# Low halves of the down-projection weights: an accumulating transfer in place of a subtraction on VectorE

## The chip, the cores and the metric

The kernel runs on one core of a Trainium2 chip. The metric is the device time of one execution in microseconds. Each time below is either that, or a time inside the one execution that the hardware profiler recorded. The engines are named as the profile names them: PE is the matrix engine (TensorE), with PEld for its weight loads, DVE is VectorE, ACT is ScalarE, POOL is GpSimd, and SP is the engine whose queue issues the transfers.

## The reference, cut to what matters

A two-layer network works on 256 rows of 1024 columns in float32. Each layer is a feed-forward, a mixer and a second feed-forward, each added to the residual `h`:

```
def swiglu(x, w_gu, w_down):              # w_gu [1024, 5632], w_down [2816, 1024]
    g, u = jnp.split(x @ w_gu, 2, axis=-1)
    return (jax.nn.silu(g) * u) @ w_down

for layer in range(2):
    h = h + 0.5 * swiglu(rmsnorm(h, ffn1_norm[layer]), ffn1_wgu[layer], ffn1_wd[layer])
    hn = rmsnorm(h, mix_norm[layer])
    h = h + (even_mixer if layer % 2 == 0 else odd_mixer)(hn, ...)
    h = h + 0.5 * swiglu(rmsnorm(h, ffn2_norm[layer]), ffn2_wgu[layer], ffn2_wd[layer])
return rmsnorm(h, final_norm)
```

So there are four feed-forwards, and each has one down-projection `w_down`. The change concerns the weights of these four products alone.

## The kernel before, in words

**Split products.** The matrix engine takes operands in a form of float32 that it handles in one pass (`F32R`) and that carries fewer bits. So each operand is split into a high and a low part, and a product is made of three: high times high, high times low, low times high. `mm3` issues them (L185, L186, L188); L186 is the one that reads the low part of the weights. For the weights the split has two steps, in `split`: ACT copies `raw` into `hi`, which rounds it (L103), and DVE writes `lo = raw - hi` (L104). The activations go through the same two lines under the tile name `aT`.

**Streaming.** All weights come from HBM in groups of 128 partitions by 2048 columns of float32, 1 MB each. `load_group` issues the transfer on SP (L123 for the gate and up weights, two transfers a group; L125 for a down-projection group, one transfer; L117 for the mixers' input projections), and then the split in pieces of 1024 columns. Three buffers hold `raw`, five hold `hi` and five hold `lo`. A `raw` buffer comes free when the group's split has read it, a `hi` or `lo` buffer when the last product with the group is done.

**Units.** A feed-forward is cut into 11 chunks of 256 of its 2816 hidden columns. For chunk j an a-unit computes gate and up (24 products of 512 columns for each half of the rows, two weight groups), applies `silu` on ACT (`ffs`, L359) and the product on DVE (`ffa`, L361); three chunks of products later two transposes on PE (L201) and another split give `aT`. A b-unit multiplies `aT` with the down-projection group of chunk j (12 products for each half of the rows) and sums in PSUM (`acc`). The order is a0, a1, b0, a2, b1, a3, b2 and so on. The 256 rows are two halves of 128, and the second half follows the first by between one and two units (`LAG`), so both use a weight group while it is in SBUF. In the middle of a feed-forward PE works through this sequence, where the number is the half of the rows: 1: a(j), 0: a(j+1), 1: b(j-1), 0: b(j), 1: a(j+1), 0: a(j+2), and so on.

**Order.** Each engine takes its instructions in a fixed order, and an instruction that waits holds up those behind it. A planner sets the order when the program is built. It goes by the order of the code and by its own reckoning of when operands and buffers will be ready, so a step that the code has later can come earlier. A few steps (transposes, norms, mixer chains) are put by hand between the products (`defer`). At the end of a feed-forward or mixer the norm needs two small operations on POOL (L223, L224).

**Buffers of a down-projection group.** Groups follow each other as a, a, b, a, a, b. With five `hi` and five `lo` buffers, the group of b(j) takes the buffers of the fifth group before it, which is the first of the two groups of a(j). They come free when the second half of the rows is halfway through a(j).

The function that the diff touches, and what calls it:

Of the kernel before, what the change touches and what calls it, by code (L numbers as in the profile page):

```python
# [25 lines left out]
EPS = 1e-6  # L26
# the first units (unit, first chunk): their loads in small pieces
FINE = {(0, 0): ((0, 1), (1, 2), (2, 4)), (0, 4): ((0, 2), (2, 4)), (1, 0): ((0, 2), (2, 4)), (1, 4): ((0, 2), (2, 4))}
# how many units the second half of the rows is behind
LAG = 1.5  # L30
# delays, in 512-column chunks of the products
FIRST = 1
# [3 lines left out]
STEPS = (2, 2, 10, 5, 3, 3, 6, 7, 3, 1, 1, 30, 10, 10, 9, 8, 3, 2, 10, 3, 3, 2, 9, 2)  # L36
# columns of the output scaled on the scalar engine
CUT = 320
# columns per splitting instruction beside the mixers
MSTEP = 512  # L40
# [12 lines left out]
def hybrid_kernel(ctx: ExitStack, tc: tile.TileContext, I, out):  # L53
# [31 lines left out]

# [1 line left out]
    xf = I["x"].rearrange("b (t p) d -> (b t) p d", p=P)  # L87
# [11 lines left out]

# [1 line left out]
    def split(src2, hi2, lo2):  # L101
        """src = hi + lo exactly, both carried by one-pass products"""
        S.activation(hi2, src2, AF.Copy)  # L103
        V.tensor_tensor(out=lo2, in0=src2, in1=hi2.bitcast(F32), op=ALU.subtract)  # L104
# [3 lines left out]

    def load_group(src, a, b, fine=False, step=1024, hook=None):
        """one streamed weight group, seen as [128, a, b] with a * b <= 2048; hook is told of each part to be split"""  # L110
        n = a * b
        raw = wpool.tile([P, n], F32, tag="raw", bufs=3, name=nm("raw"))
        if isinstance(src, list):
            rv = raw.rearrange("p (a b) -> p a b", a=a)
            c = 0
            for x in src:
                nc.sync.dma_start(rv[:, :, c:c + x.shape[2]], x)  # L117
                c += x.shape[2]
        elif len(src.shape) == 4:
            rv = raw.rearrange("p (a c b) -> p a c b", a=src.shape[1], c=src.shape[2])  # L120
            for a0, a1 in (fine or [(0, a)]):
                for c in range(src.shape[2]):
                    nc.sync.dma_start(rv[:, a0:a1, c, :], src[:, a0:a1, c, :])  # L123
        else:
            nc.sync.dma_start(raw.rearrange("p (a b) -> p a b", a=a), src)  # L125
        hi = wpool.tile([P, n], F32R, tag="hi", bufs=5, name=nm("hi"))
        lo = wpool.tile([P, n], F32R, tag="lo", bufs=5, name=nm("lo"))
        step = 512 if fine else step

        def splits():  # L130
            for c in range(0, n, step):
                e = min(n, c + step)
                with after(hook(c // step) if hook else None):
                    split(raw[:, c:e], hi[:, c:e], lo[:, c:e])
        if hook is None or hook(None):
            splits()
        else:
            defer(FIRST, splits)
        v = "p (a b) -> p a b"
        return hi.rearrange(v, a=a), lo.rearrange(v, a=a)  # L140
# [3 lines left out]
    def defer(n, fn):  # L144
        """runs fn after n more chunks of the products, or when its result is needed"""
        pend.append([n, fn])
# [15 lines left out]
    def chain(gen):  # L162
        """a chain of small steps between the chunks of the products; it yields how many chunks
        to let pass, or what has to hold, before the next step"""
        wait = [None]

        def step():
            if wait[0] is not None and not wait[0]():
                defer(1, step)
                return  # L170
            wait[0] = None
            v = next(gen, StopIteration)
            if v is StopIteration:
                return
            if callable(v):
                wait[0] = v
                v = 1
            defer(v, step)
        step()

    def mm3(outs, xT, k, wk, start, stop):
        """outs: list of (psum, column slice) sharing the stationary chunk k; wk: (hi, lo) views [128, cols]"""
        xh, xl = xT
# [12 lines left out]
    def transpose_into(src, n, xT, k0, w=None):  # L196
        """n (<= 4) chunks of 128 columns of src -> xT[:, k0 : k0 + n] in split form, times w by channel"""
        if w is None:
# [38 lines left out]
    def norm0(w):  # L237
        """the first norm, among the splits of the first weights"""
        xT = new_T(0)
# [26 lines left out]
    def norm(t, w, wait=None):  # L266
        """transposed, split, weighted residual; the row scale is left to the evacuations"""
        xT = new_T(t)
        state["xT"][t] = None

        def tr():
            # neighbouring chunks lie in different banks, which the engines then read at one time
            pt = [ps_tile(tag=x) for x in ("ps", "acc", "ps", "acc")]
# [23 lines left out]

    # the table set of the feed-forward is there before its first use
    S.activation(mh4[:, 0:1], one, AF.Silu)
    G.memset(mh4, -0.5)  # L300

    def after(ins):
        """keeps the accumulation groups of one PSUM bank in turn"""
        return tc.issue_after(ins.ins) if ins is not None else nullcontext()
# [4 lines left out]

# [1 line left out]
    def final_open():  # L311
# [3 lines left out]
    def final_part(t, n):  # L315
        """half of the row: its share of the mean square, and the product with the weights; then the scale"""
        if n == 0:
# [19 lines left out]

# [1 line left out]
    def ffn_units(wgu, wd, nxt, layer0=False):  # L339
# [31 lines left out]
        def b_unit(j):  # L371
            def load():
                return [load_group(wdv[j], 2, D)]

            def run(t, w):
# [13 lines left out]
                if j == NCHUNK - 1 and nxt is None:  # L389
                    # one half is done while the other is still in the products  # L390
                    for n in range(2):
# [20 lines left out]

# [1 line left out]
    def proj_unit(w_in, cols, body):  # L414
        """some columns of an input projection: pieces (first column, width) side by side"""
        wv = w_in.rearrange("(k p) n -> p k n", p=P)
# [42 lines left out]
    def logsigmoid(dst, z, pre, w, bufs=1):  # L459
        """min(z, 0) - log(1 + exp(-|z|))"""  # L460
        e = mt(pre + "e", [P, w], bufs)
# [5 lines left out]
    def head_rms_scale(psO, name):  # L467
        """per-head 1/rms of [128, 4, 128]"""
        sq = mt("sq", [P, 4, P], 1)
# [13 lines left out]

# [1 line left out]
    def even_units(w_in, w_lr_up, b_lr, w_out, nxt):  # L485
# [29 lines left out]
        def gla_chain(t, gl):  # L515
# [12 lines left out]
            yield STEPS[2]  # L528
            # cumulative sums by constant matrices (1/16 folded in)
            pb = ps_tile(tag="acc")  # L530
# [17 lines left out]
            yield has(t, "q", "k")  # L548
            # q exp(b - bmid), k exp(bmid - b), q exp(b), k exp(bend - b)
            q, k = d["q"], d["k"]  # L550
# [16 lines left out]
            yield STEPS[4]  # L567
            # masked scores, transposed: partitions s, columns l
            for hh in range(2):
# [181 lines left out]

# [1 line left out]
    def odd_units(w_in, prm, w_out, nxt):  # L753
# [33 lines left out]
        def softplus8():  # L787
            """8 softplus(-lambda), with log(1 + e) good for small e too"""
            lam = C["lp"][:, 2, :]
# [22 lines left out]
        def conv(x, pt, t, tag):  # L812
            """causal depthwise convolution of transposed scores; channels on partitions"""
            cb = C[x + "cb"]
# [74 lines left out]
        def ml_chain(t, u):  # L889
# [31 lines left out]
            else:  # L921
                # queries weighted by what is left of the first chunk's state
                pw = ps_tile(tag="acc")
# [15 lines left out]
            else:  # L939
                yield lambda: "mc1" in C  # L940
            # numerators, and denominators in the column of ones
            hm = mt("hm", [P, 4, P], 2)
# [42 lines left out]
        def lru_chain(t, u):  # L985
# [19 lines left out]
            S.activation(f2(r), f2(a), AF.Square)  # L1005
            # 1 - a^2 = tanh(y) (1 + a^2)
            V.scalar_tensor_tensor(out=f2(ta), in0=f2(r), scalar=1.0, in1=f2(ta), op0=ALU.add, op1=ALU.mult)
# [41 lines left out]

# [1 line left out]
    for layer in range(2):  # L1051
# [31 lines left out]

    # the second half of the rows follows LAG units behind, so that each half's small work is under the other's products
    order = [0, 1, 0, 0, 1]
# [11 lines left out]
def _constants():  # L1097
    """constants that depend on shapes alone"""
    c = {}
# [43 lines left out]
def _chan(a):  # L1143
    """[n, 512] -> [128, 4, n]: channels on partitions"""
    return np.ascontiguousarray(a.reshape(a.shape[0], 4, P).transpose(2, 1, 0))
# [29 lines left out]
```

## Time and profile before

| | |
|---|---|
| device time, median of 2 runs (lowest to highest) | 1004.94 us (1004.37 to 1005.51) |
| span of the profiled execution, first to last instruction | 1004.4 us |
| busy time of PE | 989.5 us, 99% |
| busy time of DVE | 585.9 us, 58% |
| busy time of ACT | 529.0 us, 53% |
| busy time of POOL | 22.5 us, 2% |
| busy share of the 16 DMA engines | 55.1% for the loads |

The span is one execution. It lies 0.5 us under the median of the device times and 1.1 us under the higher of the two, and a device time contains a span and the little that lies around it. "Busy" is the time in which an engine had an instruction under way. The engines work beside each other, so their busy times don't add up to the span, and what bounds the kernel is read from who waits for whom. In a row of groups the columns are line, engine, operation, tile written and tiles read, shapes, count, then total busy us and mean ns, then the idle time of the engine just before these instructions and what ended it.

### The profile page before, as it was taken

To read this page: it belongs to the slowest core of one execution; us is meant where nothing else is said; L and a number is where in the kernel's file an instruction comes from. 1 tells how busy PE (TensorE), PEld (TensorE's weight loads), DVE (VectorE), ACT (ScalarE), POOL (GpSimd) and SP (SyncE) were. 2 spreads that over 40 slices of the span, in tenths; PEclk is the share of its full clock that TensorE was granted. 3 is DMA by queue.
4 is the path that set the end of the run, shared out by engine and by line. 5 is a ranking of instruction groups with operands and counts; after the bars stand their busy time and mean duration, and the time that the engine had idled before them with its cause. 6 is when DMAs were issued, how large, how long until landed. Compare 5 with 4: busy or idle time off the path is not lost.

```text
span 1004.4 us, 12334 instructions
## 1 busy us (share of the span) xinstructions
PE 989.5 (99%) x4704; PEld 813.0 (81%) x4704; DVE 585.9 (58%) x945; ACT 529.0 (53%) x877; POOL 22.5 (2%) x54
## 2 busy tenths in 40 slices
PE   7999999999999999999999999999999999999997
PEld 5888888887888888888888888888988888888885
DVE  6654545576576654545465455545878765555453
ACT  7544444484455644444454445444998764444442
POOL 1000000000100000000000000000000000000000
PEclk9999999999999999999999999999999999999999
DMA  8956564645247565565656565655334656656521
GB/s 276 311 177 200 172 206 149 190 132 172 95 168 227 163 210 192 176 202 170 207 168 205 163 205 161 206 167 153 127 126 139 218 168 209 207 166 205 165 96 42
DMA packets 129796, 178.01 MB, mean 177 GB/s; under 512 B 8756, under 2 KB 104900, under 8 KB 129736
## 3 DMA queue, kind: packets, MB, share of 16 engines
q1 hardware_dynamic: 129736, 177.22, 55.1%
q8 instruction: 37, 0.61, 0.2%
q14 instruction: 23, 0.19, 0.1%
HBM read 176.15 MB, written 1.05 MB: 176 GB/s over the span
## 4 chain that ended last, share of the span: by engine, by line
PE 92%; ACT 3%; DMA 2%; DVE 1%; issue 1%; SPq 0%; POOLq 0%; POOL 0%; ACTq 0%
PE ps L185 19%; PE ps L188 19%; PE ps L186 19%; PE acc L185 9%; PE acc L188 9%; PE acc L186 9%; PE ps L201 2%; DMA raw<-in_ffn_wgu_dram 2%; ACT hi L103 1%; DVE lo L104 1%; DMA cum<-in_c_cum_dram 0%; PE acc L615 0%; PE acc L618 0%; PE acc L279 0%; PE acc L481 0%
## 5 line engine op out<-in xcount | busy, mean ns | idle before, releaser
L104 DVE TENSOR_TENSOR lo<-raw,hi 128x1024 fp32r<-128x1024 f32 (+3 forms) x400 | 398.8, 1029 | 262.4 <-ACT hi L103 260.8
L103 ACT ACTIVATE hi<-raw 128x1024 fp32r<-128x1024 f32 (+3 forms) x400 | 342.7, 900 | 244.5 <-PE ps L188 138.1
L185 PE MATMUL ps<-hi,Th 128*128 128x512 f32 (+3 forms) x928 | 364.2, 392 | 1.3 <-ACT Th L215 1.3
L188 PE MATMUL ps<-hi,Tl 128*128 128x512 f32 (+3 forms) x928 | 357.3, 385 | 0.0
L186 PE MATMUL ps<-lo,Th 128*128 128x512 f32 (+3 forms) x928 | 356.6, 384 | 0.0
L185 PEld LDWEIGHTS ps<-hi,Th 128*128 128x128 f32 x928 | 175.3, 189 | 34.7 <-ACT Th L215 1.7
L188 PEld LDWEIGHTS ps<-hi,Tl 128*128 128x128 f32 x928 | 175.0, 189 | 34.6 <-issue 0.2
L186 PEld LDWEIGHTS ps<-lo,Th 128*128 128x128 f32 x928 | 175.5, 189 | 31.8 <-DVE lo L104 0.2
L185 PE MATMUL acc<-hi,aT 128*128 128x512 f32 x352 | 142.7, 405 | 0.0
L186 PE MATMUL acc<-lo,aT 128*128 128x512 f32 x352 | 138.9, 394 | 0.0
L359 ACT ACTIVATE ffs<-ps,rs 128x256 f32<-128x256 f32 x88 | 41.8, 474 | 154.0 <-PE ps L188 154.0
L188 PE MATMUL acc<-hi,aT 128*128 128x512 f32 x352 | 111.0, 395 | 0.0
L361 DVE SCALAR_TENSOR_TENSOR ffa<-ps,rs,ffs 128x256 f32<-128x256 f32 x88 | 42.4, 481 | 92.4 <-ACT ffs L359 92.4
L188 PEld LDWEIGHTS acc<-hi,aT 128*128 128x128 f32 x352 | 66.1, 188 | 15.1
L186 PEld LDWEIGHTS acc<-lo,aT 128*128 128x128 f32 x352 | 66.5, 189 | 13.8
L185 PEld LDWEIGHTS acc<-hi,aT 128*128 128x128 f32 x352 | 66.5, 189 | 13.4
L104 DVE TENSOR_TENSOR aT<-ps,aT 128x256 fp32r<-128x256 f32 x88 | 36.8, 418 | 7.5 <-ACT aT L103 7.5
L103 ACT ACTIVATE aT<-ps 128x256 fp32r<-128x256 f32 x88 | 32.8, 373 | 11.6 <-PE ps L201 11.6
L201 PEld LDWEIGHTS ps<-ident,ffa 128*128 128x128 f32 x176 | 24.6, 140 | 12.3 <-DVE ffa L361 0.6
L201 PE MATMUL ps<-ident,ffa 128*128 128x128 f32 x176 | 33.6, 273 | 0.1
L215 ACT ACTIVATE Th<-ps,nw 128x128 fp32r<-128x128 f32 x56 | 21.0, 375 | 12.9 <-PE ps L279 11.3
L185 PE MATMUL acc<-hi,Th 128*128 128x512 f32 x64 | 25.3, 399 | 0.0
(269 smaller groups left out, 535.9 us busy)
## 6 DMA issues: line engine op xcount, KB each, us to landing
raw<-in_ffn_wgu_dram SPq DMA_DIRECT2D x168, 512.0 KB, 4.9
raw<-in_ffn_wd_dram SPq DMA_DIRECT2D x44, 1024.0 KB, 4.9
raw<-in_e_w_in_dram SPq DMA_DIRECT2D x13, 1024.0 KB, 5.0
raw<-in_o_w_in_dram SPq DMA_DIRECT2D x9, 1024.0 KB, 5.1
raw<-in_e_w_out_dram SPq DMA_DIRECT2D x4, 1024.0 KB, 5.0
raw<-in_o_w_out_dram SPq DMA_DIRECT2D x4, 1024.0 KB, 5.0
raw<-in_ffn_wgu_dram SPq DMA_DIRECT2D x14, 256.0 KB, 6.3
rope<-in_c_rope_dram SPq DMA_DIRECT2D x4, 256.0 KB, 3.9
```

Source lines behind the costliest of these rows:

```text
L103: S.activation(hi2, src2, AF.Copy)
L104: V.tensor_tensor(out=lo2, in0=src2, in1=hi2.bitcast(F32), op=ALU.subtract)
L185: T.matmul(ps, xh[:, k, :], wk[0][:, sl], start=start, stop=False)
L186: T.matmul(ps, xh[:, k, :], wk[1][:, sl], start=False, stop=False)
L188: state["mm"] = T.matmul(ps, xl[:, k, :], wk[0][:, sl], start=False, stop=stop)
L201: T.transpose(pt[:, i * P:(i + 1) * P], src[:, i * P:(i + 1) * P], ident)
L215: last = S.activation(hi, p_, AF.Copy, scale=w[:, k:k + 1])
L359: state["act"] = S.activation(s, ps[:, :FCH], AF.Silu, scale=rs)
L361: state["dve"] = V.scalar_tensor_tensor(out=a, in0=ps[:, FCH:], scalar=rs, in1=s, op0=ALU.mult, op1=ALU.mult)
```

## The change

For the 44 down-projection groups `load_group` gets `accum=True`. ACT then copies the whole group of 2048 columns into `hi` in one instruction, and writes `lo = -hi` with a second copy of the same size. A transfer issued on POOL's queue then adds `raw` to `lo` in place, from SBUF to SBUF, so that `lo` becomes `raw - hi`. DVE has no part in it. The other weight groups are split as before. Comments and docstrings also leave the file; nothing else changes.

```
-    def load_group(src, a, b, fine=False, step=1024, hook=None):
+    def load_group(src, a, b, fine=False, step=1024, hook=None, accum=False):
...
         hi = wpool.tile([P, n], F32R, tag="hi", bufs=5, name=nm("hi"))
         lo = wpool.tile([P, n], F32R, tag="lo", bufs=5, name=nm("lo"))
         step = 512 if fine else step
+        if accum:
+
+            S.activation(hi, raw, AF.Copy)
+            S.activation(lo, hi.bitcast(F32), AF.Copy, scale=-1.0)
+            G.dma_start(lo, raw, accum_op=ALU.add)
+            v = "p (a b) -> p a b"
+            return hi.rearrange(v, a=a), lo.rearrange(v, a=a)
...
         def b_unit(j):
             def load():
-                return [load_group(wdv[j], 2, D)]
+                return [load_group(wdv[j], 2, D, accum=True)]
```

## The prediction

> **What bounds the kernel now.** I read the profile's page first, for the busy times, the queues and the chain that ended last.
>
> ```profile
> PE 989.5 (99%) x4704; PEld 813.0 (81%) x4704; DVE 585.9 (58%) x945; ACT 529.0 (53%) x877; POOL 22.5 (2%) x54
> ...
> q1 hardware_dynamic: 129736, 177.22, 55.1%
> ...
> PE 92%; ACT 3%; DMA 2%; DVE 1%; issue 1%; SPq 0%; POOLq 0%; POOL 0%; ACTq 0%
> ...
> raw<-in_ffn_wd_dram SPq DMA_DIRECT2D x44, 1024.0 KB, 4.9
> ```
>
> PE is busy for 989.5 of 1004.4 us, and the chain that ended last runs through PE for 92%. DVE, which the change relieves, is 1% of that chain. All idle time of PE together is 14.9 us, 1.5% of the span, so relief for another engine can't win 2% even if it removed all of it. The question is only whether the change makes PE wait. I take 2% (20 us) as what a measurement of this kernel tells from no change.
>
> Next I read the groups by shape and one period in the middle of the last feed-forward: the sums of the stretch, and in order of time ACT, DVE, SP and PE.
>
> ```profile
> L104 DVE TENSOR_TENSOR lo<-raw,hi 128x1024 fp32r<-128x1024 f32 x256 | 305.7, 1221 | 233.2 <-ACT hi L103 232.0 <-DMA raw<-in_ffn_wd_dram 1.0
> L103 ACT ACTIVATE hi<-raw 128x1024 fp32r<-128x1024 f32 x256 | 260.9, 1053 | 214.7 <-PE ps L188 120.1 <-PE acc L188 86.1 <-DMA raw<-in_ffn_wgu_dram 3.6
> L103 ACT ACTIVATE hi<-raw 128x512 fp32r<-128x512 f32 x136 | 76.8, 627 | 16.7 <-PE ps L188 9.5 <-DMA raw<-in_ffn_wgu_dram 5.4 <-issue 1.6
> ```
>
> ```profile
> 845.00:861.94 16.94, 16.94 (x80) 13.88 (x77) 8.63 (x10) 7.41 (x10) 0.00 (x0) 1.00 0.59 187
> ```
>
> ```profile
> 850.76 2.01 ACT L103 ACTIVATE hi<-raw 128x1024 fp32r<-128x1024 f32 x2 [3.44 <-PE ps L188]
> 853.48 0.48 ACT L359 ACTIVATE ffs<-ps,rs 128x256 f32<-128x256 f32 x1 [0.71 <-PE ps L188]
> 853.85 2.00 ACT L103 ACTIVATE hi<-raw 128x1024 fp32r<-128x1024 f32 x2
> ...
> 861.98 1.06 ACT L103 ACTIVATE hi<-raw 128x1024 fp32r<-128x1024 f32 x1 [2.33 <-PE acc L188]
> ...
> 867.70 2.01 ACT L103 ACTIVATE hi<-raw 128x1024 fp32r<-128x1024 f32 x2 [3.44 <-PE ps L188]
> ```
>
> ```profile
> 851.85 2.36 DVE L104 TENSOR_TENSOR lo<-raw,hi 128x1024 fp32r<-128x1024 f32 x2 [3.03 <-ACT hi L103]
> 854.13 0.48 DVE L361 SCALAR_TENSOR_TENSOR ffa<-ps,rs,ffs 128x256 f32<-128x256 f32 x1
> 854.93 2.36 DVE L104 TENSOR_TENSOR lo<-raw,hi 128x1024 fp32r<-128x1024 f32 x2 [0.33 <-ACT hi L103]
> ```
>
> ```profile
> 854.24 0.37 SPq L125 DMA_DIRECT2D raw<-in_ffn_wd_dram  x1
> 857.32 9.39 SPq L123 DMA_DIRECT2D raw<-in_ffn_wgu_dram  x4
> ```
>
> ```profile
> 847.84 0.39 PE L185 MATMUL ps<-hi,Th 128*128 128x512 f32 x1
> ...
> 853.28 0.39 PE L185 MATMUL ps<-hi,Th 128*128 128x512 f32 x1
> ```
>
> ```profile
> 855.32 0.38 PE L201 MATMUL ps<-ident,ffa 128*128 128x128 f32 x2
> ```
>
> ```profile
> 861.91 0.48 PE L185 MATMUL acc<-hi,aT 128*128 128x512 f32 x1
> 862.23 0.39 PE L186 MATMUL acc<-lo,aT 128*128 128x512 f32 x1
> ```
>
> The period is 16.94 us (850.76 to 867.70), and PE has no gap in it. In it a down-projection group b(j) goes this way. At 850.76 ACT begins its high part; what ended ACT's wait is a product (L188), because the group's `hi` and `lo` buffers are those that the first half of a(j) gives back then. The transfer of the next down-projection group starts at 854.24, just after the two subtractions ended (851.85 + 2.36 = 854.21), which marks these splits as b(j)'s. PE reads the low part first at 862.23. So `lo` is ready 8.0 us early. That slack, not DVE's busy time, is what the change spends.
>
> **The change part by part.** *Removed:* two subtractions of 1.22 us per group on DVE, 44 x 2.44 = 107 us of busy time. They lie beside PE's products, so the end gains nothing.
>
> *ACT.* From the rows of 512 and 1024 columns, 1024 more columns cost 2 x (1.053 - 0.627) = 0.85 us, so one of 2048 costs 1.053 + 0.85 = 1.9 us. Two 1024-column copies (2.01 us) become two of 1.9 us, 3.8 in all: ACT has 1.8 us more per group and its share of the period goes from 7.41 to 9.2 of 16.94 us, which fits. From 850.76 the negated copy is done at 854.57. Behind it on ACT waits `ffs`, which ran at 853.48 and now runs at 854.57, 1.09 us later. Its result goes through `ffa` (done at 854.61) to the transposes at 855.32, a cover of 0.71 us. What shows through is between nothing and 1.09 - 0.71 = 0.38 us a period. I take nothing, because the planner orders by readiness: it had the splits at 853.85 ahead of work that the code has earlier, and it can put one product ahead of the transposes. The splits behind move to about 855.0; the buffer for them is free and their group is read a period later.
>
> *The transfer.* It may start at 854.57 and must have landed by 862.23, a cover of 7.66 us. No transfer of this kind is in the trace, so I bound it by the loads.
>
> ```profile
> DMA to landing us min/median/max: 4.6/4.9/7.7
> ```
>
> ```profile
> L224 POOL TENSOR_TENSOR rs<-rm,mh 128x1 f32<-128x1 f32 x12 | 6.6, 553 | 1.0
> ...
> L224 POOL TENSOR_TENSOR rs<-rm,mh 128x4 f32<-128x4 f32 x6 | 6.1, 1013 | 0.5
> ```
>
> ```profile
> POOL rm L223 <- ACT junk L234: 628.3, 11, 179.0
> ```
>
> The loads kept 16 engines busy for 55.1% of 1004.4 us with 177.22 MB, so 3.12 us per MB, and 3.3 us for a group of 128 x 2048 x 4 bytes = 1.05 MB. A load of that size lands after 4.9 us, so 1.6 us are start and completion. An adding transfer reads two operands and writes one. Counted once, like a load, it lands after 4.9 us; with both operands read at that price after 1.6 + 6.5 = 8.2; with the write on top after 11.4. I take two reads, since a load's price contains its write. Issuing it on POOL costs between 0 and 1.0 us, by the POOL rows; I take 0.55, the smaller operation. Sharing the engines with a load costs between 0 and 3.3 us, one load's worth; I take 0, since 3.12 us per MB was measured on packets that already share. Together 8.2 + 0.55 = 8.7 us from the negated copy, against a cover of 7.66: PE waits 1.1 us at the first product with `lo`. It waits in order, so the other half's products stand behind it, and nothing gives the time back: the buffers of the next group come free by PE's own progress.
>
> By the Trainium skill, page "Collectives: The Full Stack", section "The bandwidth ceiling: the fold count and why AG ≠ RS ≠ AR", a reducing transfer runs at half the rate of a copy because each chunk needs two source reads, not because the addition costs anything; that is a rule against this change, and no run here shows it yet.
>
> *The `raw` buffer* is given back when the transfer has landed, at 854.57 + 8.7 = 863.3 in place of 854.21. If the next down-projection group loads into the same buffer it lands at 863.3 + 4.9 = 868.2, when its split would begin at 867.70, plus the 1.1 us that PE lost by then: just in time. The loop of one buffer, 3.8 + 8.7 + 4.9 + 0.37 for the issue = 17.8 us, stays under the new period of 18.0. SP's queue is in order, so the two loads at 857.32 and after may stand behind the wait for that buffer; their groups are split from 861.98 and 870.8 on (one period after 853.85), so this costs nothing while the transfer is under about 11 us.
>
> *POOL's queue* has only the norms' small operations, and it sat waiting for ACT's sums of squares for 628.3 us. A norm can now stand behind a transfer that waits for ACT's two copies: between nothing and 3.8 us at each of the 12 in the row of 128x1, 46 us. I take nothing, because a steady period has no POOL operation (0.00 in the sums above) and only a transfer beside a norm could hold one up.
>
> *Sum.* Of 44 groups, the first of each feed-forward is split beside a norm and its cover is another, so I count 40: 40 x (8.7 - 7.66) = 42 us. Made against the profiled execution: 1004.4 + 42 = 1046; it lies 0.5 us under the median of the runs, so 1047.
>
> **The rivals.**
> *The transfer hides (not slower).* Place: the wait of L186 in each b-unit. It decides at 7.66 us from the negated copy to the landing. For it: counted once it takes 4.9 + 0.55 = 5.5 us, and reading SBUF may be quicker than HBM. Also, the planner may foresee a late `lo` and put the other half's a-unit first: that has 24 products of weights that are already split, 5.4 us of cover more (847.84 to 853.28, the first products of two a-units that follow each other). Against it: two operands. The time is then the old one, 1005 us.
> By the Trainium skill, page "DMA: Bandwidth & Descriptors", section "Anatomy of one DMA — SWDGE (gpsimd) path", a transfer issued from POOL's queue costs about 2.0 us plus its bytes at 436 GB/s. With both operands' bytes that is an estimate of 6.8 us, by which the transfer would hide; for one load's bytes it gives 4.4 us, where the trace's loads from SP's queue took 4.9.
>
> *ACT alone costs.* The transfer hides, but `ffs` pushes the transposes by 0.38 us in 40 periods: 15 us, 1020 us. For it: copies of 1.9 us can't be interrupted. Against it: the planner.
>
> *Far longer transfer.* At 11.4 us with write and reads apart, and up to 3.3 more beside a load: 40 x (11.4 - 7.66) = 150 to 40 x (14.7 - 7.66) = 282 us, so 1155 to 1287 us. The `raw` loop gives the same order: with the longest landing in the trace, 7.7 us, it is 20.6 us, 3.7 more than the period, 1152 us. For it: the engines are already busy for 0.59 of a period. Against it: this needs each byte to cost three times.
>
> *Something gets faster.* Only PE's 14.9 us of idle time are there, so over 2% needs what no row shows.
>
> **How the numbers follow.** Late by 0.5 to 3.5 us in 40 periods, 1025 to 1145 us: 0.43, the likeliest, with 1047 as its value. Hidden: 0.37. ACT alone: 0.07. Far longer: 0.11. Faster by over 2%: 0.02. The range from 1003 to 1145 holds the first three and leaves out 0.13. Slower by over 2% is 0.43 + 0.11 = 0.54, within 2% is 0.37 + 0.07 = 0.44, faster 0.02.
>
> **What would show it.** The forecast: PE idle before L186 with `acc`, ended by a DMA, about 40 times and 1 us each; a period of about 18 us; a new queue with 44 transfers, landing 8 to 9 us after issue. Two ACT copies of 1.9 us in a row and `ffs` about 1.1 us later in its period show the ACT step. If the landing is under 7.5 us, or the order on PE has changed so that the a-unit runs ahead of the b-unit, the forecast is wrong and the time is the old one. If idle time ended by a DMA stands before L103 in place of L186, the `raw` loop bounds and not the cover.

## The result and the profile after

The changed kernel takes 1066.18 us (median of 2 runs, 1065.18 to 1067.17) against 1004.94 us: a ratio of 1.061, 95% interval 1.058 to 1.064, so 61 us more. The profiled execution of it has a span of 1063.4 us, 59.0 more than before.

The rows of the page that answer to those shown of before: the busy times, the queues, the chain that ended last by engine, and the landing of the transfers.

```profile
PE 1014.2 (95%) x4704; PEld 817.9 (77%) x4704; DVE 486.0 (46%) x857; ACT 603.8 (57%) x877; POOL 60.3 (6%) x98
...
q1 hardware_dynamic: 129736, 177.22, 49.2%
q0 software_dynamic: 6336, 46.14, 24.0%
...
PE 47%; DMA 31%; issue 16%; ACT 4%; DVE 1%; SPq 0%; POOLq 0%; POOL 0%; ACTq 0%
...
raw<-in_ffn_wd_dram SPq DMA_DIRECT2D x44, 1024.0 KB, 7.1
lo<-raw POOLq DMA_DIRECT2D x44, 1024.0 KB, 7.9
```

DVE lost 100 us of busy time, and nothing came of it. PE, which had 14.9 us without an instruction under way, now has 49.2. A quarter of the time of the DMA engines is the new queue, and DMA has gone from 2% of the chain to 31%.

The waits name the place. The columns are who waited for what, the total in us, the times, and the longest.

```profile
PEld acc L193 <- DMA lo<-raw: 37.8, 33, 5.5
PE acc L193 <- DMA lo<-raw: 27.2, 32, 5.1
```

L193 is the line that was L186: the product with the low part of the weights. One period in the last feed-forward, in order of time on ACT, POOL and PE:

```profile
900.45 1.92 ACT L131 ACTIVATE hi<-raw 128x2048 fp32r<-128x2048 f32 x1 [4.14 <-PE ps L195]
902.39 1.92 ACT L132 ACTIVATE lo<-hi 128x2048 fp32r<-128x2048 f32 x1
904.22 0.45 ACT L366 ACTIVATE ffs<-ps,rs 128x256 f32<-128x256 f32 x1
...
918.12 1.92 ACT L131 ACTIVATE hi<-raw 128x2048 fp32r<-128x2048 f32 x1 [4.09 <-PE ps L195]
```

```profile
904.61 0.86 POOL L133 DMA_DIRECT2D lo<-raw  x1 [16.83 <-ACT lo L132]
```

```profile
911.68 0.48 PE L192 MATMUL acc<-hi,aT 128*128 128x512 f32 x1
912.54 0.50 PE L193 MATMUL acc<-lo,aT 128*128 128x512 f32 x1 [0.37 <-DMA lo<-raw]
```

From the start of the high copy to the issue of the transfer pass 4.16 us, and 7.9 us later, at 912.5, it has landed. PE stands at L193 and starts at 912.54. The product with the high part came 0.86 us before it; in the kernel before, 0.32 us (861.91 and 862.23). So 0.54 us are lost at this product, and the period is 17.67 us in place of 16.94; the other 0.2 us lie at the product right behind it (0.34 us to the next start in place of 0.24) and at the transposes.

### The profile page after: what moved, and what is told of

It reads as the page before. It is cut to its first block, busy times and chain, and to the rows that moved or that the text cites. A ratio compares the mean times of both kernels' runs of the same rounds, so it can differ in the third digit from the quotient of the medians.

```text
span 1063.4 us, 12402 instructions
## 1 busy us (share of the span) xinstructions
PE 1014.2 (95%) x4704; PEld 817.9 (77%) x4704; DVE 486.0 (46%) x857; ACT 603.8 (57%) x877; POOL 60.3 (6%) x98
## 3 DMA queue, kind: packets, MB, share of 16 engines
q1 hardware_dynamic: 129736, 177.22, 49.2%
## 4 chain that ended last, share of the span: by engine, by line
PE 47%; DMA 31%; issue 16%; ACT 4%; DVE 1%; SPq 0%; POOLq 0%; POOL 0%; ACTq 0%
DMA lo<-raw 28%; PE ps L192 9%; PE ps L193 9%; PE ps L195 8%; PE acc L193 6%; PE acc L195 5%; PE acc L192 5%; DMA raw<-in_ffn_wgu_dram 1%; ACT hi L103 1%; DVE lo L104 1%; DMA raw<-in_ffn_wd_dram 1%; ACT hi L131 1%; DMA raw<-in_o_w_in_dram 1%; DMA raw<-in_e_w_in_dram 0%; PE acc L286 0%
## 5 line engine op out<-in xcount | busy, mean ns | idle before, releaser
L104 DVE TENSOR_TENSOR lo<-raw,hi 128x1024 fp32r<-128x1024 f32 (+3 forms) x312 | 294.7, 975 | 172.4 <-ACT hi L103 172.1
L193 PE MATMUL ps<-lo,Th 128*128 128x512 f32 (+3 forms) x928 | 361.0, 389 | 0.0
L103 ACT ACTIVATE hi<-raw 128x1024 fp32r<-128x1024 f32 (+3 forms) x312 | 253.8, 856 | 131.8 <-PE acc L195 85.8
L193 PEld LDWEIGHTS ps<-lo,Th 128*128 128x128 f32 x928 | 176.3, 190 | 32.2 <-DVE lo L104 0.2
L131 ACT ACTIVATE hi<-raw 128x2048 fp32r<-128x2048 f32 x44 | 84.3, 1916 | 167.9 <-PE ps L195 162.4
L193 PE MATMUL acc<-lo,aT 128*128 128x512 f32 x352 | 145.7, 415 | 27.3 <-DMA lo<-raw 27.2
L192 PE MATMUL acc<-hi,aT 128*128 128x512 f32 x352 | 145.1, 414 | 0.0
L195 PE MATMUL acc<-hi,aT 128*128 128x512 f32 x352 | 114.5, 405 | 0.0
L193 PEld LDWEIGHTS acc<-lo,aT 128*128 128x128 f32 x352 | 68.2, 194 | 52.1 <-DMA lo<-raw 37.8
L132 ACT ACTIVATE lo<-hi 128x2048 fp32r<-128x2048 f32 x44 | 84.3, 1916 | 1.1
L195 PEld LDWEIGHTS acc<-hi,aT 128*128 128x128 f32 x352 | 68.2, 194 | 16.1
L192 PEld LDWEIGHTS acc<-hi,aT 128*128 128x128 f32 x352 | 67.8, 193 | 12.3
L133 POOL DMA_DIRECT2D lo<-raw x44 | 38.4, 873 | 664.4 <-ACT lo L132 636.6
L208 PE MATMUL ps<-ident,ffa 128*128 128x128 f32 x176 | 35.9, 286 | 3.3 <-DVE ffa L368 3.3
```

The source lines that it names most:

```text
L131: S.activation(hi, raw, AF.Copy)
L132: S.activation(lo, hi.bitcast(F32), AF.Copy, scale=-1.0)
L133: G.dma_start(lo, raw, accum_op=ALU.add)
L192: T.matmul(ps, xh[:, k, :], wk[0][:, sl], start=start, stop=False)
L193: T.matmul(ps, xh[:, k, :], wk[1][:, sl], start=False, stop=False)
L195: state["mm"] = T.matmul(ps, xl[:, k, :], wk[0][:, sl], start=False, stop=stop)
```

## The experiments

The theory at the start was that PE waits in order for the landing (1). The rivals were the long copies on ACT, which hold up the silu and the transposes (2), and the added bytes on the DMA engines, which slow the loads (3).

**ACT's part alone.** The copies stay and DVE does the addition.

```
-            G.dma_start(lo, raw, accum_op=ALU.add)
+            V.tensor_tensor(out=lo, in0=raw, in1=lo.bitcast(F32), op=ALU.add)
```

> ScalarE's part alone: both whole-group copies stay, VectorE adds raw to the negated copy, no transfer from POOL. If PE waits for the landing of the transfer (theory 1), its waits for lo are gone; what is left is the silu 1.1 us late and 0.3 us before the transposes in some 40 periods, so 1005 to 1018 us. If the long copies on ScalarE are the cause (theory 2), most of the loss stays: 1045 us or more. If the load on the DMA engines is the cause (theory 3: slower weight loads, a slower start), 1005 us and the loads land after 4.9 us again.

Measured: 1009.22 us, ratio 1.0044 (1.0029 to 1.0059). One period on ACT, and the wait at the transposes:

```profile
869.65 1.92 ACT L131 ACTIVATE hi<-raw 128x2048 fp32r<-128x2048 f32 x1 [3.44 <-PE ps L195]
...
886.68 1.92 ACT L131 ACTIVATE hi<-raw 128x2048 fp32r<-128x2048 f32 x1 [3.45 <-PE ps L195]
```

```profile
PEld ps L208 <- DVE ffa L368: 10.8, 36, 0.3
```

The late silu shows at the transposes 36 times, but each period is only 0.09 us longer (17.03), and the whole loss is 4.5 us. ACT is a small part, and theory 2 falls.

**The transfer in two pieces.**

```
-            S.activation(hi, raw, AF.Copy)
-            S.activation(lo, hi.bitcast(F32), AF.Copy, scale=-1.0)
-            G.dma_start(lo, raw, accum_op=ALU.add)
+            for c in (0, 1024):
+                e = slice(c, c + 1024)
+                S.activation(hi[:, e], raw[:, e], AF.Copy)
+                S.activation(lo[:, e], hi[:, e].bitcast(F32), AF.Copy, scale=-1.0)
+                G.dma_start(lo[:, e], raw[:, e], accum_op=ALU.add)
```

> The group in two pieces of 1024 columns: high copy, negated copy and transfer of the first piece, then of the second. The first transfer starts 1.7 us earlier and is half as long, so it should land about 4 us before its use, and the second, needed 1.4 us later, about when it is needed. Theory 1 (PE waits for the landing): the waits for lo nearly vanish, 1005 to 1025 us. Theory 2 (ScalarE): the two engines' copies take longer in all (4.2 in place of 3.8 us), so no gain, 1066 us or more. Theory 3 (bytes on the DMA engines): the same bytes, 1055 to 1066 us.

Measured: 1025.47 us, ratio 1.020 (1.019 to 1.022), which is at the upper end of theory 1 (0.5 us above it) and 30 us under theory 3. PE waits for `lo` at 2 products in place of 32. Two steady periods (columns: stretch, its length, busy us and count of PE, PEld, DVE, ACT and POOL, granted clock, DMA share, GB/s):

```profile
877.00:893.95 16.95, 16.95 (x78) 13.89 (x77) 6.36 (x9) 9.19 (x13) 1.71 (x2) 1.00 0.90 248
893.95:910.90 16.95, 16.95 (x78) 13.89 (x77) 6.36 (x9) 9.19 (x13) 1.72 (x2) 1.00 0.90 249
```

The same bytes move, the DMA engines are busy for 0.90 of the period where it was 0.59, and PE has no gap. So the share of busy DMA engines costs nothing in itself in these periods, and theory 3 falls for them. 21 us are left elsewhere.

**The copies in pieces, one transfer.**

```
-            S.activation(hi, raw, AF.Copy)
-            S.activation(lo, hi.bitcast(F32), AF.Copy, scale=-1.0)
+            for c in (0, 1024):
+                S.activation(hi[:, c:c + 1024], raw[:, c:c + 1024], AF.Copy)
+            for c in (0, 1024):
+                S.activation(lo[:, c:c + 1024], hi[:, c:c + 1024].bitcast(F32), AF.Copy, scale=-1.0)
             G.dma_start(lo, raw, accum_op=ALU.add)
```

> The four copies on ScalarE have 1024 columns each, and one transfer of the whole group follows. The silu can slip in ahead of the last copy, so the transposes come in time, but the transfer starts 0.4 to 0.9 us later. Theory 1 (PE waits for the landing): 0.4 to 0.9 us more in some 40 periods, less the 0.3 us at the transposes: 1070 to 1090 us. Theory 2 (long copies on ScalarE): 1045 to 1055 us. Theory 3 (bytes on the DMA engines): 1066 us.

Measured: 1086.87 us, ratio 1.081 (1.079 to 1.083). One period on ACT, POOL and PE:

```profile
973.60 2.01 ACT L132 ACTIVATE hi<-raw 128x1024 fp32r<-128x1024 f32 x2 [4.69 <-PE ps L197]
```

```profile
978.16 0.86 POOL L135 DMA_DIRECT2D lo<-raw  x1 [17.33 <-ACT lo L134]
```

```profile
986.17 0.47 PE L195 MATMUL acc<-lo,aT 128*128 128x512 f32 x1 [0.93 <-ACT aT L103]
```

The issue comes 4.56 us after the first copy, 0.4 later than after the change, and the gap in PE grows from 0.37 to 0.93. The transfer lands 7.88 us after issue, at 986.04, and PE goes on 0.13 us later. This view puts 28 such waits down to `aT` and 9 to the transfer, because a copy of ACT ends at nearly the same time (985.79 + 0.37). But PE also starts 0.13 us after the landing where that copy had ended 0.7 us before (landing at 913.38, start at 913.51), so it is the landing that PE waits for. The silu was earlier and the kernel slower, against theory 2.

**The negation on DVE.** ACT makes the high copies as before the change; DVE multiplies them by -1 in pieces of 1024; one transfer.

```
-            S.activation(hi, raw, AF.Copy)
-            S.activation(lo, hi.bitcast(F32), AF.Copy, scale=-1.0)
+            for c in (0, 1024):
+                S.activation(hi[:, c:c + 1024], raw[:, c:c + 1024], AF.Copy)
+                V.tensor_scalar(out=lo[:, c:c + 1024], in0=hi[:, c:c + 1024].bitcast(F32), scalar1=-1.0, scalar2=None,
+                                op0=ALU.mult)
```

> The negated copy is made by VectorE in pieces of 1024 columns, beside ScalarE's next high copy; the transfer of the whole group is the same. It starts 0.6 us or more earlier, and ScalarE is as free as before the change. Theory 1 (PE waits for the landing): the wait of 0.4 us a period vanishes except where a load runs beside the transfer, 1010 to 1035 us. Theory 2 (ScalarE): nearly the old time, 1005 to 1010 us. Theory 3 (bytes on the DMA engines): 1055 to 1066 us.

Measured: 1029.24 us, ratio 1.024 (1.022 to 1.026). The issue comes 3.26 us after the start of the first copy:

```profile
906.70 2.01 ACT L132 ACTIVATE hi<-raw 128x1024 fp32r<-128x1024 f32 x2 [4.37 <-PE ps L197]
```

```profile
909.96 0.86 POOL L135 DMA_DIRECT2D lo<-raw  x1 [17.02 <-DVE lo L133]
```

```profile
PE acc L195 <- DMA lo<-raw: 11.0, 8, 6.5
```

PE waits 8 times in place of 32, and one wait of 6.5 us, at the first transfer of the program, is more than half of it. That is theory 1 again. The waits make 11 of the 24.5 us; 10.2 us at half clock around that first wait and the ends of the feed-forwards, both treated below, have a part in the rest.

**What the addition costs.** Two kernels move the same 1 MB from `raw` to `lo` and leave out the addition, so that `lo` holds `raw`; one issues the transfer from POOL, the other from SP.

```
-            G.dma_start(lo, raw, accum_op=ALU.add)
+            G.dma_start(lo, raw)
```
```
+            nc.sync.dma_start(lo.bitcast(F32), raw)
```

> The same transfer from POOL without the addition (lo becomes raw, so that the low parts are wrong): one operand is read in place of two. If the second read makes the length, it lands 2.5 to 3.3 us earlier (about 5 us after issue), PE's waits for lo vanish and the time is 1010 to 1030 us. If the issue, the start and the completion make it, or the rate of the writing side, it lands after 7 us or more and the time stays near 1066 us.

> A plain copy of the same bytes issued from SP in place of POOL's adding transfer (lo becomes raw, so that the low parts are wrong). It measures a transfer of this size between two SBUF buffers with neither POOL nor addition: 4 to 5 us to landing if one read and one write go at the loads' rate. The time says little, since the copy's wait for ScalarE now stands in SP's queue ahead of the loads: 1005 to 1040 us.

Measured: 1013.32 us from POOL, ratio 1.008 (1.006 to 1.011), and 1009.42 us from SP, ratio 1.004 (1.003 to 1.006). The new queue and the landing (min, median and max) without the addition, from POOL:

```profile
q0 software_dynamic: 6336, 46.14, 11.8%
...
DMA to landing us min/median/max: 4.1/4.2/7.9
```

and from SP:

```profile
lo<-raw SPq DMA_DIRECT2D x44, 1024.0 KB, 4.6
```

Same packets and bytes as with the addition, but 11.8% of 1010.3 us over 44 transfers is 2.7 us of all 16 engines for each, where 24.0% of 1063.4 us is 5.8. With nothing beside the transfer it is 5.2 (57.7% of the 9 us from 358 on, with one transfer alone in them). So adding about doubles the engines' time, and the median landing is 7.9 us in place of 4.2, 3.7 us and not 2.5 to 3.3 as expected. POOL as the issuer isn't what is dear: the copy from SP lands after 4.6. Adding takes a second read and an addition together, and no run tells the one from the other.

**Every second group.** `accum=j % 2 == 0`, 24 of 44 groups.

> The change for every second down-projection group (even chunks), 24 of 44; the others by subtraction. If each period pays its own wait (theory 1), the steady part of the loss about halves: 0.74 us in some 20 periods in place of 40, with the start kept, 1030 to 1045 us. If it is a matter of throughput (the DMA engines or the loop of a raw buffer can't keep up with a transfer every period), the free period between makes it good: 1010 to 1025 us.

Measured: 1030.01 us, ratio 1.026 (1.023 to 1.029).

```profile
PE acc L193 <- DMA lo<-raw: 15.4, 17, 5.5
```

PE waits 17 times in place of 32. The median distance of two transfers is 34.65 us where two old periods are 33.88, so a transfer costs 0.77 us in a middle period, whether or not the next one follows at once; with all of them it was 0.78 (17.72, the median of 36 distances of the transfers' issues, less 16.94). So in the middle periods it is no matter of throughput.

**The start and the ends.** What the pieces left (21 us) was tried in two steps, both with the transfer in two pieces as above: the first two groups of the program by subtraction, then also the last two groups of each feed-forward.

```
-                return [load_group(wdv[j], 2, D, accum=True)]
+                return [load_group(wdv[j], 2, D, accum=not (layer0 and j < 2))]
```
```
+                return [load_group(wdv[j], 2, D, accum=j < NCHUNK - 2 and not (layer0 and j < 2))]
```

> The transfer in two pieces, and the first two down-projection groups of the first feed-forward of the program by subtraction, as before the change. If what the pieces left (21 us, 13.5 of them before the end of the first feed-forward) is the start, where the loads alone keep the DMA engines nine tenths busy and the adding transfer is in their way, the time is 1010 to 1016 us. If it is spread over all periods, it is 1023 us or more.

> As with pieces and the first two groups by subtraction, and now also the last two groups of each feed-forward by subtraction: 34 of 44 groups are left to the transfer, all in the middle of a feed-forward. If what is left (11 us) comes from the ends, where the transfers keep two of the three raw buffers, the next stage's first weights load late, and the update of h on VectorE stands behind their splits, the time is 1004 to 1008 us. If the middle periods still cost something, 1011 us or more.

Measured: 1016.33 us, ratio 1.011 (1.010 to 1.013), and then 1004.94 us, ratio 0.9996 (0.9986 to 1.0005). The first was forecast for the whole remainder and brought 9 us of it; the second brought the other 11. The end of the first feed-forward in the first of the two, on ACT, DVE and PE:

```profile
189.24 1.21 ACT L103 ACTIVATE hi<-raw 128x544 fp32r<-128x544 f32 x2 [5.93 <-DMA raw<-in_e_w_in_dram]
...
193.02 2.19 ACT L103 ACTIVATE hi<-raw 128x512 fp32r<-128x512 f32 x4 [2.21 <-DMA raw<-in_e_w_in_dram]
```

```profile
193.68 1.90 DVE L104 TENSOR_TENSOR lo<-raw,hi 128x512 fp32r<-128x512 f32 x3 [1.99 <-ACT hi L103]
195.49 0.68 DVE L396 SCALAR_TENSOR_TENSOR h<-acc,h 128x512 f32<-128x512 f32 x1
```

```profile
194.03 0.63 PE L197 MATMUL acc<-hi,aT 128*128 128x512 f32 x2
196.23 0.33 PE L288 MATMUL ps<-ident,h 128*128 128x128 f32 x1 [1.57 <-DVE h L396]
```

What SP's queue waited for in the same run before the loads of the mixer's weights (L117), from 165 to 200 us (total in us, times, longest):

```profile
SPq L117 <- DMA lo<-raw: 15.1, 2, 10.6
```

ACT waits for the load of the mixer's weights. The last two down-projection groups follow each other closely and hold two of the three `raw` buffers until their transfers have landed, so that load starts late: the second group of these weights is issued at 181.43, and at 174.79 without the last two transfers. The subtractions for those weights come late on DVE, the update of `h` stands behind them in DVE's order, the norm's transposes wait for `h`, and PE idles for 1.57 us. From 197.4 to 200.8 the granted clock is halved behind it, which costs up to 1.7 us more. Without the last two transfers the same update ran at 193.81 and not at 195.49, and no gap is left. With 34 of 44 groups still going through the transfer, the kernel is as fast as before and not faster.

## Why the prediction was right

The forecast was 1047 us for a transfer that lands late in each middle period; it came out at 1066, slower as said, by the mechanism given 0.43. Its steps, one by one:

- *Relief of DVE wins nothing.* Right: the kernel with 34 transfers has an interval of 0.9986 to 1.0005.
- *ACT.* Two copies of 1.92 us (1.9 forecast), silu right behind the negated copy. What shows through was put between 0 and 0.38 us a period, and taken at 0; ACT alone measured 0.09.
- *The transfer: mis-sized in its parts, not far off in sum.* From the end of the negated copy to the landing 8.7 us were forecast: 0.55 for the issue, 1.6 for start and completion, 6.5 for two reads, 0 for sharing. Measured are 8.2: 0.3 from the copy's end (904.31) to the issue on POOL, 1.8 for start and completion (7.0 less 5.2, with nothing beside the transfer), 5.2 on the engines, and 0.9 beside the usual loads. Of the three bounds the one with two reads was right: the engines' time doubles against the same transfer without the addition. The price of a read was too high: loads out of HBM take 3.3 us for this size, the transfer inside SBUF without the addition 2.7. By the Trainium skill, page "Collectives: The Full Stack", section "The bandwidth ceiling: the fold count and why AG ≠ RS ≠ AR", a reducing transfer runs at about half the rate of a copy (measured there 1.93) because it reads two sources, and not because adding costs anything. The traces here agree with the size, 5.2 against 2.7 us of the engines, and no run here shows which of the two makes it.
- *Contention, taken at 0.* Too low. A transfer with nothing beside it (the first row, from 358 to 367 us) landed after 7.0 us. The usual one, with 0.26 MB of loads beside it (issued at 904.61), took 7.9. The slow ones, with 0.3 to 2.1 MB of loads or another adding transfer beside them, took 8.0 to 10.7, as the stretch of the last feed-forward from 1010.5 to 1021 us shows:

```profile
lo<-raw POOLq DMA_DIRECT2D x1, 1024.0 KB, 7.0
```

```profile
raw<-in_ffn_wd_dram SPq DMA_DIRECT2D x2, 1024.0 KB, 4.9
lo<-raw POOLq DMA_DIRECT2D x1, 1024.0 KB, 9.7
```

```profile
1018.26 0.48 PE L192 MATMUL acc<-hi,aT 128*128 128x512 f32 x1
1020.95 0.50 PE L193 MATMUL acc<-lo,aT 128*128 128x512 f32 x1 [2.22 <-DMA lo<-raw]
```

- *The cover of 7.66 us.* Right: from the negated copy to the landing passed 8.18 us (904.31 to 912.49), and less the 0.54 lost at L193 that is 7.64. The same budget explains the runs. From the high copy's start to the first low product were 11.47 us before the change (850.76 to 862.23). The change needs 4.16 + 7.9 = 12.06 and is 0.6 late; the copies in pieces need 4.56 + 7.9 = 12.46 and are 1.0 late (a gap of 0.93); the negation on DVE needs 3.26 + 7.9 = 11.16 and waits only where the landing takes 8.7 us or more; without the addition it is 4.16 + 4.2 = 8.36, and PE waits once.
- *40 periods of 1.06 us, 42 us.* The product came out lower and the rest, counted at nothing, made it up. There are 36 distances of about a period: at the median's excess of 0.78 that is 28 us, and the few long ones add 17. The other 14 of the 59 us lie at the start and at the ends of the feed-forwards (the first of the 36, 20.4 us, belongs to the start too). The forecast of about 40 waits of 1 us each came out as 32, most of them 0.34 to 0.49 us long. A part that nobody had counted is the clock: 6.8 us at half clock at the start and five stretches of 3.4 us behind later waits cost up to 12 of the 59 us (last section). So the mechanism was right in the middle periods, and that 1047 comes as near to 1066 as it does is in part luck.
- *The `raw` buffer at nothing.* Right in the middle, wrong at the ends, where the forecast looked at no next stage: this is a step that failed. Removing the last two transfers of each feed-forward won 11 us in the kernel with pieces.
- *The first groups.* They were left out of the count because their cover is another. In the first feed-forward of the program it is a worse one: the first transfer landed only after 10.7 us, among the loads of the start, and PE stood for 5.1 us. The other three feed-forwards show no wait at their first group. The program's first two groups by subtraction won 9 us in the kernel with pieces.
- *The rivals.* Hidden (0.37): no, though by 0.6 us only. With nothing beside it the transfer lands 7.3 us after the negated copy (0.3 + 7.0), inside the cover of 7.66; beside the usual loads it is 8.2, so the loads decided. By the Trainium skill, page "DMA: Bandwidth & Descriptors", section "Anatomy of one DMA — SWDGE (gpsimd) path", the estimate for both operands' bytes was 6.8 us, which fits the undisturbed 7.0. The planner kept the b-unit's place in the middle periods and didn't put the other half first; only in the first b-unit of the program did it put ten products of an a-unit ahead of the low ones, and PE waited 5.1 us all the same. ACT alone (0.07): its own time is 1009, not 1020. Far longer (0.11): no, the longest transfer landed after 10.7 us, under the 11.4 of this rival.

## What to carry to other kernels

A step that an engine with time to spare does in 1.2 us pieces can be moved off it at a loss: what counts is the slack between the end of the old step and the first use, here 8 us, against what the replacement takes longer in all. As measured here, price an adding transfer at twice the engine time of a copy of the same bytes, add its start and the loads beside it, and cut it into pieces in the order of use if it must be hidden. Then look at the ends of a stage: a source buffer that is held for 8 us longer delays the next stage's first load.

## What the runs showed of the hardware

The granted clock of TensorE is lower after the change, and it wasn't in the forecast.

```profile
core 0: 1063.4 us, clock 0.985
```

A span of 1063.4 us at 0.985 is short of 16 us of full clock, and one of 1004.4 at 0.996 of 4, so at most 12 us of the loss are the clock. About 1.2 us after the wait of 2.22 us shown above, the clock is halved for one stretch of 3.4 us (PEclk, third column from the right, 0.50 in the second row):

```profile
1018.60:1022.10 3.50, 1.28 (x6) 0.97 (x6) 2.69 (x3) 2.00 (x3) 0.00 (x0) 1.00 0.79 282
1022.10:1025.50 3.40, 3.40 (x10) 2.65 (x9) 0.00 (x0) 0.00 (x0) 0.00 (x0) 0.50 0.86 302
1025.50:1028.90 3.40, 3.40 (x17) 2.76 (x16) 0.00 (x0) 0.75 (x1) 0.00 (x0) 1.00 0.00 0
```

PE did 10 products there and 17 in the next 3.4 us. So a wait of about 2 us can cost 1.7 us more. The shorter waits of 0.4 us are followed by full clock. But so is a wait of 2.58 us that ended at 422.7, so the length alone doesn't decide:

```profile
417.94:421.36 3.42, 2.20 (x11) 1.52 (x9) 0.55 (x1) 1.64 (x3) 0.00 (x0) 1.00 0.84 228
421.36:424.77 3.41, 2.05 (x9) 1.69 (x10) 2.14 (x3) 0.64 (x1) 0.00 (x0) 1.00 0.56 189
424.77:428.18 3.41, 3.41 (x17) 2.82 (x16) 0.00 (x0) 0.00 (x0) 0.00 (x0) 1.00 1.04 346
```

The trace shows what goes with it. Its half-clock stretches behind waits in the later part begin at 513.5, 544.2, 609.1, 749.0 and 1022.1 us, and the distances between them are 9, 19, 41 and 80 times 3.413 us: they lie on one grid. In the cell of that grid just ahead of each, PE had no instruction for 1.84 to 2.22 us. The wait of 2.58 us was cut by a line of the grid (421.36 in the rows above) into 1.2 and 1.4 us. A wait of 1.64 us that lay in one cell (127.8 to 131.2) wasn't followed by half clock, while 1.70 us in one cell of the kernel in pieces (205.7 to 209.1) was. So in these traces, from 15 us on where their record of the clock begins, half clock follows where the idle time within one cell of 3.41 us reaches some 1.7 us. One more stretch, at 803.6, follows no idle time; the kernel before has it too (at 754.6), and it stays unexplained. No run was made to test this.

An adding transfer of 1 MB inside SBUF takes 5.2 us of the 16 engines and 7.0 us to landing with nothing beside it, against 2.7 and 4.2 without the addition.
